# Seven-product up projection: relu on ScalarE, sums on VectorE, a fixed order on four engines, and the norm factor moved to the down sum

## The chip, the cores and the metric

One program on one core of a Trainium2 chip. The metric is the time of one execution on the device, in microseconds (us). The engines are called as the profile calls them: PE (TensorE matmul), PEld (its weight load), DVE (VectorE), ACT (ScalarE), POOL (GpSimd) and SP (SyncE, which issues nearly all DMA transfers here). Each engine works through its own instructions strictly in order, and they wait for each other on semaphores.

## The reference, cut to what matters

A trunk of two layers over 1040 positions of 1024 channels, batch 1, in float32. Layer 0 mixes by differential attention, layer 1 by a short convolution. Each mixer is followed by an MLP with 4096 hidden channels, and the change is in the MLP:

```python
def _rmsnorm(x, g):
    return x * lax.rsqrt(jnp.mean(x * x, -1, keepdims=True) + 1e-6) * g

def _sqrelu_mlp(h, w_up, w_down):
    a = jax.nn.relu(jnp.einsum('bld,df->blf', h, w_up))
    return jnp.einsum('blf,fd->bld', a * a, w_down)

for i in range(2):
    h = _rmsnorm(hres, norm_g[i, 0])
    m = mixer[i](h)                              # attention, then short convolution
    hres = hres + _rmsnorm(m, norm_g[i, 1])
    h = _rmsnorm(hres, norm_g[i, 2])
    hres = hres + _rmsnorm(_sqrelu_mlp(h, w_up[i], w_down[i]), norm_g[i, 3])
```

The factor of the norm in front of the MLP, written rs here, is one positive number for each position. The hidden value is (relu(u)·rs)² with u the projection of the unscaled row, and this equals relu(u)²·rs². So rs can be applied before the square, or rs² at any later point up to the sum over the hidden channels.

## The kernel before

Channels lie on the 128 partitions, positions along the free axis. A float32 product is made of three PE products of rounded parts: a value is split into `hi` (a rounded copy, made on ACT) and `lo` (the rest, subtracted on DVE), and PE sums hi·hi, hi·lo and lo·hi in PSUM.

The MLP of a layer (`mlp`) goes through these stages:

1. **Boundary groups** (`up_plain` with `boundary=True`): the first 4 of 32 hidden blocks of 128, by plain products, while the norm in front of the MLP is still being finished (`norm_step`, L390 to L393).
2. **Plain up groups** (`up_plain`): 4 more hidden blocks. Behind each product L465 takes relu and rs from PSUM to SBUF on DVE, L466 squares on ACT, L467 and L468 split, and two DMAs write the parts to `plain_dram`. Between the groups `turn` (called through `between`) forms sums and differences of the four quarters of the input by `sums` (L475 to L478) on POOL.
3. **Up by seven products** (`UpSevens`): the other 24 hidden blocks in 12 steps q, two blocks each. In a step seven products of half size take the place of eight (a Strassen-like scheme: rows and columns in halves, seven products of sums). The weights of a step come in two raw tiles (L526), POOL forms four sums of them (L534 to L537), ACT and DVE split them (L520, L521). The seven products go to the PSUM chains `a`, `b`, `c` (`ua`, `ub`, `uc`). Out of PSUM, three partial sums are copied by ACT (L603), the others added by DVE (L611); then relu and rs on DVE (L587, L606), square on ACT (L588, L607). The result is a tile `f` of eight slots; `finish` forms four sums of its slots on POOL (L571 to L574), since the down projection is done by seven products too, splits seven slots (L577 on ACT, L579 on DVE) and writes 14 parts to `seven_dram` (L578, L580). There are two buffers for f, called `two`, used by even and odd q in turn.
4. **Down plain**: the 4 plain up groups, loaded back into `stage` (L835), times four weight tiles, g = 0 to 3 (`load_weights`, `down_plain`, PE L188 `dn`). L841 copies out of PSUM into the accumulator `acc`, whose two tiles lie in the memory of the two f buffers.
5. **Down by seven products** (`Sevens`): 24 steps in 6 blocks b of 4. The operands of block 0 go to tiles `HH` and `HL` in layer 0, `YHa`, `YHb` and `HL` in layer 1 (`load`, L676), those of later blocks to `fx` and the same tiles in turn. L767 adds each product to `acc` on DVE.
6. The boundary groups' part of the down sum, with the last norm.

What sets the order: within one engine the order is the scheduler's, which places instructions by their readiness and by the order of the program text; inside the blocks `tc.manual_schedule(engines={PE})` of `UpSevens.run` and `Sevens.run` PE alone follows the text. All DMAs here are issued by SP in one order, and a DMA whose source is not ready holds those behind it. Names with a number such as `w_raw_11529` are tiles; `[waits ...]` lists the engines and DMA channels (DMAHW0 to DMAHW7) that an instruction waits for.

## Time and profile before

| | before |
|---|---|
| median of 3 runs | 2464.67 us (2463.58 to 2465.43) |
| profiled execution: its own time | 2467.3 us |
| profiled execution: span of the core | 2465.5 us |
| PE busy | 2315.0 us, 94% |
| DVE, ACT, POOL busy | 1644.1, 1114.4, 771.0 us |
| DMA moved | 374.63 MB |

The trace comes from the profiled execution, whose span lies 1.8 us inside its own time. Times inside the trace are counted from the start of the span. The seven-product up stage runs from about 727 to 998 us in layer 0 and from about 1832 to 2104 us in layer 1; the plain down stage follows it for some 60 us, and the seven-product down stage after that.

Where rows of the "stretches" view are quoted, the columns are: stretch, its length, then busy us and instructions of PE, PEld, DVE, ACT and POOL, then the clock granted to PE, the share of the DMA engines and GB/s. In the "waits" view a row has the engine and line that waits, what it waited for, the sum in us, the number of times and the longest.

### The profile page before, as it was taken

The page shows a single profiled execution, that of the slowest core. Times are in us where ns is not written, and L with a number is a line of the kernel's source. Part 1 is how long each engine was busy: PE and PEld are TensorE (multiplying, and loading weights), DVE is VectorE, ACT ScalarE, POOL GpSimd, SP SyncE. Part 2 cuts the span into 40 slices and gives each one's busy share as a digit, 9 for nine tenths or more (in the row PEclk, how much of TensorE's full clock was granted, in tenths as well). Part 3 has the DMA queues.
Part 4 walks back from the last instruction along what each step waited for, and adds up shares of the span by engine and source line. Part 5 has one row for each costly group of instructions (what it writes and reads, how often), then busy time and mean ns, then how long its engine had stood idle before and what let it go on. Part 6 is the DMA issues. An engine that isn't in the chain of part 4 may idle for free. (4 is left out here: it accounts for less than half of the span.)

```text
span 2465.5 us, 38542 instructions
## 1 busy us (share of the span) xinstructions
PE 2315.0 (94%) x14474; PEld 2162.6 (88%) x14474; DVE 1644.1 (67%) x2815; ACT 1114.4 (45%) x2141; POOL 771.0 (31%) x662
## 2 busy tenths in 40 slices
PE   8999999999889988799999999999899988899997
PEld 7899999999889988799999899999777666688887
DVE  7887777755977677267666944423976667367766
ACT  6777777765545455322123522224544445322224
POOL 3211111105614445133324200004624555133326
PEclk9999999999999999899999999999999999899998
DMA  4212222432445665875733311122445666876652
GB/s 133 63 55 61 61 61 61 146 106 90 133 144 173 217 213 203 324 281 198 276 131 102 128 50 46 46 73 72 135 154 173 217 215 210 313 284 221 246 196 69
DMA packets 168779, 374.63 MB, mean 152 GB/s; under 512 B 17040, under 2 KB 73744, under 8 KB 168080
## 3 DMA queue, kind: packets, MB, share of 16 engines
q1 hardware_dynamic: 168592, 372.17, 44.0%
q8 instruction: 114, 1.87, 0.3%
q14 instruction: 73, 0.60, 0.1%
HBM read 234.34 MB, written 129.24 MB: 147 GB/s over the span
## 5 line engine op out<-in xcount | busy, mean ns | idle before, releaser
L151 DVE TENSOR_TENSOR w_lo<-w_raw,w_hi 128x1024 fp32r<-128x1024 f32 (+1 forms) x63 | 82.6, 1313 | 153.1 <-ACT w_hi L150 153.0
L213 POOL TENSOR_TENSOR mss<-mss,sq 128x344 f32<-128x344 f32 (+2 forms) x42 | 50.1, 1197 | 375.8 <-ACT sq L212 372.6
L150 ACT CAST w_hi<-w_raw 128x1024 fp32r<-128x1024 f32 (+2 forms) x87 | 89.8, 1033 | 154.2 <-DMA w_raw<-in_wall 64.9
L722 POOL TENSOR_TENSOR s_tmp<-w_raw 128x256 f32<-128x256 f32 x48 | 35.7, 745 | 391.4 <-DVE s_lo L715 234.6
L188 PE MATMUL up<-HL,w_hi 128*128 128x344 f32 (+3 forms) x352 | 120.9, 345 | 9.4 <-DVE HL L393 9.4
L521 DVE TENSOR_TENSOR us_lo<-t,us_hi 128x1024 fp32r<-128x1024 f32 x48 | 60.6, 1263 | 100.7 <-ACT us_hi L520 100.6
L714 ACT CAST s_hi<-s_tmp 128x1024 fp32r<-128x1024 f32 x48 | 50.4, 1050 | 163.6 <-PE pb L744 154.4
L151 POOL TENSOR_TENSOR w_lo<-w_raw,w_hi 128x1024 fp32r<-128x1024 f32 (+1 forms) x24 | 57.5, 2395 | 196.6 <-ACT w_hi L150 183.9
L1396 ACT ACTIVATE E<-E,mn 16x16 f32<-16x16 f32 (+5 forms) x144 | 105.3, 732 | 24.1 <-DVE mn L1391 23.5
L188 PE MATMUL dn<-stage,w_hi 128*128 128x344 f32 (+2 forms) x320 | 91.0, 372 | 24.3 <-ACT w_hi L150 19.7
L188 PE MATMUL mo<-HL,w_hi 128*128 128x342 f32 (+2 forms) x312 | 99.9, 320 | 0.0
L1391 DVE CUSTOM_DVE_ANT_0 E<-s,G 16x16 f32<-16x16 f32 (+5 forms) x144 | 64.4, 455 | 39.9 <-PE s L1387 37.4
L188 PEld LDWEIGHTS dn<-stage,w_hi 128*128 128x128 f32 x320 | 61.5, 203 | 32.7 <-ACT w_hi L150 20.4
L579 DVE TENSOR_TENSOR f<-f,fhi 128x512 fp32r<-128x512 f32 x84 | 74.1, 931 | 22.7 <-ACT fhi L577 22.7
L714 ACT CAST a_hi<-w_raw 128x512 fp32r<-128x512 f32 x48 | 29.8, 620 | 129.5 <-DMA w_raw<-in_wall 126.8
L767 DVE TENSOR_TENSOR acc<-acc,pa 128x512 f32<-128x512 f32 x96 | 65.8, 686 | 33.5 <-PE pa L744 31.7
L188 PEld LDWEIGHTS up<-HL,w_hi 128*128 128x128 f32 x352 | 68.0, 193 | 16.4 <-DVE HL L393 13.0
L534 POOL TENSOR_TENSOR t<-w_raw 128x512 f32<-128x512 f32 x24 | 31.6, 1315 | 148.6 <-DMA w_raw<-in_wall 119.8
L715 DVE TENSOR_TENSOR s_lo<-s_tmp,s_hi 128x1024 fp32r<-128x1024 f32 x48 | 58.8, 1224 | 23.6 <-ACT s_hi L714 23.6
L562 PE MATMUL ua<-x,us_hi 128*128 128x256 f32 (+2 forms) x288 | 67.2, 326 | 7.7 <-ACT us_hi L520 2.1
L520 ACT CAST us_hi<-t 128x1024 fp32r<-128x1024 f32 x48 | 50.1, 1046 | 52.5 <-POOL t L535 46.1
L1139 PE MATMUL q<-HH,w_hi 128*128 128x348 f32 (+1 forms) x192 | 65.1, 339 | 6.5 <-ACT w_hi L150 6.5
(716 smaller groups left out, 9205.6 us busy)
## 6 DMA issues: line engine op xcount, KB each, us to landing
w_raw<-in_wall SPq DMA_DIRECT2D x189, 512.0 KB, 3.7
seven_dram<-fhi SPq DMA_DIRECT2D x84, 257.0 KB, 4.3
fx<-seven_dram SPq DMA_DIRECT2D x42, 514.0 KB, 7.2
seven_dram<-fhi SPq DMA_DIRECT2D x84, 256.0 KB, 2.7
seven_dram<-f SPq DMA_DIRECT2D x84, 256.0 KB, 4.7
fx<-seven_dram SPq DMA_DIRECT2D x42, 512.0 KB, 6.9
HH<-seven_dram SPq DMA_DIRECT2D x21, 514.0 KB, 7.7
HL<-seven_dram SPq DMA_DIRECT2D x21, 514.0 KB, 8.3
```

The lines of the kernel that those rows point to most:

```text
L150: nc.scalar.copy(hi_part, raw[:, cols])
L151: (eng or nc.vector).tensor_sub(lo_part, raw[:, cols], hi_part.bitcast(F32))
L188: nc.tensor.matmul(ps, lhs[:, a:b], rhs(k, cols), start=n == 0, stop=n == last)
L521: nc.vector.tensor_sub(hl[1], src, hl[0].bitcast(F32))
L562: nc.tensor.matmul(ps[:, off : off + n], lhs[:, a : a + P], self.operand(slot, t, j)[:, c : c + n], start=first and k == 0, stop=k == 11, ...
L579: nc.vector.tensor_sub(v[slot].bitcast(F32R), v[slot], hi.bitcast(F32))
L714: nc.scalar.copy(hl[0], src)
L715: nc.vector.tensor_sub(hl[1], src, hl[0].bitcast(F32))
L767: nc.vector.tensor_add(am, am, got)
L1139: nc.tensor.matmul(ps, wh[:, a], self.HH[:, k, s], start=k == 0, stop=False)
L1391: nc.vector.tensor_tensor_reduce(out=e[:rows, p0 : p0 + n], in0=ps[:rows], in1=self.G[:rows, off : off + n], scale=-(2.0 ** -(h + 1)), sca ...
L1396: nc.scalar.activation(e[:rows, :ext], e[:rows, :ext], AF.Exp, scale=-1.0, bias=mn, accum_out=H["sums"][:rows, c : c + 1])
```

## The change

It has seven parts.

1. In `UpSevens.run` the fixed order of the program text now holds for PE, ACT, DVE and POOL, where it held for PE alone. The text is rewritten so that the work on the tile of step q−1 and the stores of steps q−2 and q−1 are spread over the products of step q.
2. Relu moves from DVE (with rs) to ACT (without rs), in the plain up groups and in the steps q < 10. The boundary groups and the steps 10 and 11 keep rs. In exchange rs² is formed once after the up stage, and 16 products on DVE per layer (`nc.vector.tensor_mul(am, am, rs2...)`) scale the accumulator in the last steps of down block 4, which is behind all that lacks rs and ahead of all that has it.
3. The four sums of f's slots, and `turn`'s sums, move from POOL to DVE.
4. The second raw weight tile has two places (the second is `spare`, a tile of the norm that is free by then), both halves are fetched at the start of a step, and the four weight sums come in two pairs.
5. The stores of a tile are issued one by one in fixed places, no longer all after `finish`.
6. The two f buffers are taken once for the stage (`f586a` and `f586b` in layer 0), no longer anew in each step.
7. Down plain: the weights of g = 0 and 1 are loaded and split, and g = 2 loaded, ahead of the loads of `stage`; g = 3 follows after g = 0; the operands of block 0 are loaded two slots after each g.

```diff
@@ up_plain
-                    nc.vector.scalar_tensor_tensor(r, ps, 0.0, rs[:, s], ALU.max, ALU.mult)
+                    if boundary:
+                        nc.vector.scalar_tensor_tensor(r, ps, 0.0, rs[:, s], ALU.max, ALU.mult)
+                    else:
+                        nc.scalar.activation(r, ps, AF.Relu)
@@ UpSevens
-            sums(nc.gpsimd, t1, t3, t4, t2)
+            sums(nc.vector, t1, t3, t4, t2)
...
+        def fetch(self, q):
+            raws = []
+            for half in range(2):
+                i = self.base + 2 * q + half
+                if half and q % 2:
+                    raw = self.raws[1][:, :1024]
+                else:
+                    raw = (self.wu if half else wp).tile([P, 1024], F32, tag="w_raw", name=f"w_raw{i}", bufs=1)
+                nc.sync.dma_start(raw, wall[i])
+                raws.append(raw)
...
+            if step == 0:
+                nc.gpsimd.tensor_add(t[:, n:], a21, a22)
+                nc.gpsimd.tensor_sub(t[:, :n], t[:, n:], a11)
+            else:
+                nc.gpsimd.tensor_sub(t[:, :n], a11, a21)
+                nc.gpsimd.tensor_sub(t[:, n:], a12, self.W[q]["t21"][:, :n])
...
-            nc.gpsimd.tensor_sub(v[3], v[7], v[0])
-            nc.gpsimd.tensor_sub(v[2], v[5], v[3])
-            nc.gpsimd.tensor_sub(v[4], v[5], v[7])
-            nc.gpsimd.tensor_sub(v[6], v[1], v[2])
-            for slot in (0, 3, 5, 4, 2, 1, 6):
...
+        def store(self, q, slot):
+            x = self.v[q % 2][:, slot]
+            hi = self.fp.tile([P, self.H], F32R, tag="hi", name=f"fhi{q}_{slot}_{count[0]}", bufs=4)
+            nc.scalar.copy(hi, x)
+            nc.sync.dma_start(self.spool[q][:, slot, 0], hi.bitcast(F32))
+            nc.vector.tensor_sub(x.bitcast(F32R), x, hi.bitcast(F32))
+            nc.sync.dma_start(self.spool[q][:, slot, 1], x)
...
+            def closed(slot, q):
+                at, z = {1: (0, 0), 4: (5, 1), 5: (7, 1), 6: (1, 0)}[slot]
+                x = self.v[q % 2][:, at]
+                src = sums[slot, q] if slot == 6 else x
+                if q < 2 * (NW - 1):
+                    nc.scalar.activation(x, src, AF.Relu)
                 else:
+                    nc.vector.scalar_tensor_tensor(x, src, 0.0, self.rs[:, z * H : (z + 1) * H], ALU.max, ALU.mult)
+                nc.scalar.activation(x, x, AF.Square)
...
-            with tc.manual_schedule(engines={mybir.EngineType.PE}):
+            with tc.manual_schedule(engines={ET.PE, ET.Activation, ET.DVE, ET.Pool}):
                 step(0, 0)
+                for q in range(n + 2):
+                    if more:
+                        self.fetch(q + 1)
                     step(4, q - 1)
+                    if 0 < q < n:
+                        self.settle(q, "s21")
+                    self.store(q - 2, 2)
                     step(5, q - 1)
+                    added(4, q - 1)
+                    self.store(q - 2, 1)
+                    closed(4, q - 1)
+                    step(1, q)
+                    held(0, q)
+                    added(5, q - 1)
+                    self.store(q - 2, 6)
+                    closed(5, q - 1)
+                    step(6, q - 1)
+                    added(1, q)
+                    if more:
+                        self.settle(q + 1, "a")
+                        self.combine(q + 1, 0)
+                    closed(1, q)
+                    sub(q - 1, 3, 7, 0)
+                    step(2, q)
+                    closed(6, q - 1)
+                    sub(q - 1, 4, 5, 7)
+                    sub(q - 1, 2, 5, 3)
+                    self.settle(q, "s34")
+                    step(3, q)
+                    held(2, q)
+                    sub(q - 1, 6, 1, 2)
+                    self.store(q - 1, 0)
+                    self.store(q - 1, 3)
+                    if more:
+                        self.combine(q + 1, 1)
+                    step(0, q + 1)
+                    held(3, q)
+                    self.settle(q, "d")
+                    self.store(q - 1, 5)
+                    self.store(q - 1, 4)
@@ Sevens.run
                 nc.vector.tensor_add(am, am, got)
+                if slot in (1, 4, 5, 6) and q // 4 == NW - 2:
+                    nc.vector.tensor_mul(am, am, rs2[:, z * H : (z + 1) * H])
@@ mlp
-        up.run(m)
+        up.run()
+        rs = rs[:, :W]
+        nc.vector.tensor_mul(rs, rs, rs)
...
+        ws, split, slots = [weights(), weights()], load_weights(), iter(range(7))
         for c0, n in chunks:
             for i in range(2):
                 nc.sync.dma_start(f[i][:, :, s].bitcast(F32), plain[1][:, i * FB : (i + 1) * FB, s])
-        for slot in range(7):
-            seven.load(0, slot)
         for g in range(FB):
-            down_plain(acc, *f, [g], chunks, lambda mi, cols, am, ps: nc.scalar.copy(am, ps))
+            w = ws[g]
+            down_plain(acc, *f, [g], chunks, lambda mi, cols, am, ps: nc.scalar.copy(am, ps), [[(w, 0), (w, FB * P)]])
+            for slot in (next(slots, None) for _ in range(2)):
+                if slot is not None:
+                    seven.load(0, slot)
+            if split:
+                ws.append(split())
+                split = load_weights() if g == 0 else None
```

Here `sub(q, out, a, b)` subtracts slot b from slot a of the tile of step q on DVE, `held` is the copy of a partial sum on ACT, and `added` the addition of a product on DVE, both as before.

**In the steady state of the up stage**, POOL had the four sums of f between the weight sums. Before, in layer 0:

```order
L571 TENSOR_TENSOR f_2a<-f_2a 128x514 [waits DMAHW1_49,DMAHW5_49,DMAHW0_49,Activation_49]
L573 TENSOR_TENSOR f_2a<-f_2a 128x514
L572 TENSOR_TENSOR f_2a<-f_2a 128x514 [waits Pool_49]
L574 TENSOR_TENSOR f_2a<-f_2a 128x514 [waits Activation_49,Pool_49]
L534 TENSOR_TENSOR t_4_597_9354<-w_raw_9352 128x512 [waits DMAHW4_49,DVE_49]
L536 TENSOR_TENSOR t_4_597_9355<-w_raw_9191,w_raw_9352 128x512 [waits DMAHW2_49,DVE_49]
L535 TENSOR_TENSOR t_4_597_9354<-t_4_597_9354,w_raw_9191 128x512 [waits Pool_49]
L537 TENSOR_TENSOR t_4_597_9355<-w_raw_9191,t_4_597_9354 128x512 [waits Pool_49]
```

After, the same sums stand on DVE (L634), among the additions from PSUM (L617), the splits of the weights (L527) and the splits of f (L591):

```order
L617 TENSOR_TENSOR f586b<-f586b,uc_9236 128x514 [waits PE_49]
L527 TENSOR_TENSOR ua_lo_597_9296<-w_raw_9167,ua_hi_597_9295 128x1024 [waits DMAHW7_49,Activation_49]
L634 TENSOR_TENSOR f586a<-f586a 128x514 [waits DMAHW6_49]
L634 TENSOR_TENSOR f586a<-f586a 128x514 [waits DMAHW4_49]
L634 TENSOR_TENSOR f586a<-f586a 128x514 [waits DVE_49]
L527 TENSOR_TENSOR us_lo_597_9334<-t_3_595_9124,us_hi_597_9333 128x1024 [waits Activation_49]
L634 TENSOR_TENSOR f586a<-f586a 128x514 [waits DMAHW2_49,DVE_49]
L591 TENSOR_TENSOR f586a<-f586a,fhi_0_598_9364 128x514 [waits Activation_49]
L591 TENSOR_TENSOR f586a<-f586a,fhi_3_598_9369 128x514 [waits Activation_49]
```

The sums have left POOL and now stand in DVE's fixed order, one tile behind the additions.

**At the end of the up stage in layer 0**, SP issued the last stores of the tile of step 10 (`f_10a`) ahead of the loads of `stage` (L835) and of block 0 (L676). Before:

```order
L578 DMA seven_dram_81<-fhi_6_621_11345 128x514 [waits DMAHW5_49,Activation_49]
L580 DMA seven_dram_81<-f_10a 128x514 [waits DMAHW6_49,DVE_49]
L580 DMA seven_dram_81<-f_10a 128x514 [waits DMAHW7_49,DVE_49]
L580 DMA seven_dram_81<-f_10a 128x514 [waits DMAHW0_49,DVE_49]
L578 DMA seven_dram_81<-fhi_0_622_11489 128x514 [waits DMAHW1_49,Activation_49]
L835 DMA stage_11529<-plain_dram_1_78 128x4x344 [waits DMAHW2_49,PE_49]
```

After, the last two parts of that tile (slot 6, from `fhi_6` and `f586a`) stand behind the loads of `stage` (L887; the last of them is the first row) and behind eight loads of block 0 (L721):

```order
L887 DMA stage_11514<-plain_dram_1_78 128x4x340 [waits DMAHW5_49]
L721 DMA HH<-seven_dram_81 128x1028 [waits DMAHW6_49,PE_49]
L721 DMA HL<-seven_dram_81 128x1028 [waits DMAHW7_49]
L721 DMA HH<-seven_dram_81 128x1028 [waits DMAHW0_49,PE_49]
L721 DMA HL<-seven_dram_81 128x1028 [waits DMAHW1_49]
L721 DMA HH<-seven_dram_81 128x1028 [waits DMAHW2_49]
L721 DMA HL<-seven_dram_81 128x1028 [waits DMAHW3_49]
L721 DMA HH<-seven_dram_81 128x1028 [waits DMAHW4_49,PE_49]
L721 DMA HL<-seven_dram_81 128x1028 [waits DMAHW5_49]
L590 DMA seven_dram_81<-fhi_6_622_11436 128x514 [waits DMAHW6_49,Activation_49]
L592 DMA seven_dram_81<-f586a 128x514 [waits DMAHW7_49,DVE_49]
L721 DMA HH<-seven_dram_81 128x1028 [waits DMAHW0_49]
```

The store of slot 6 has moved from ahead of these loads to behind most of them; in layer 1 it stands behind all 14 loads of block 0 and a weight load.

**On ACT at the same place** the first copy of the plain down stage (L890, which was L841) waits for that store, since `acc0a` lies in the memory of `f586a`:

```order
L589 CAST fhi_3_622_11478<-f586b 128x514 [waits DMAHW7_49,Activation_49]
L589 CAST fhi_5_622_11483<-f586b 128x514 [waits DMAHW1_49,Activation_49]
L589 CAST fhi_4_622_11488<-f586b 128x514 [waits DMAHW6_49,DVE_49,Activation_49]
L890 COPY acc0a<-dn_11537 128x344 [waits DMAHW5_49,DMAHW2_49,DMAHW7_49,DMAHW0_49,PE_49]
L890 COPY acc0a<-dn_11551 128x344 [waits PE_49]
```

All further copies of the first accumulator tile, the splits of the weights of g = 2 and 3 and the last splits of f stand behind that one wait on ACT.

More of the change, by code (lines that the diff above doesn't have):

```diff
@@ L614, in run, with held, added @@
-            with tc.manual_schedule(engines={mybir.EngineType.PE}):
+                sums[slot, q] = self.product(tiles[chain, q], slot, q, first)
+            def held(slot, q):
+                if 0 <= q < n:
+                    nc.scalar.copy(self.v[q % 2][:, {0: 0, 2: 7, 3: 5}[slot]], sums[slot, q])
+            def added(slot, q):
+                if 0 <= q < n and slot != 6:
+                    x = self.v[q % 2][:, {1: 0, 4: 5, 5: 7}[slot]]
+                    nc.vector.tensor_add(x, x, sums[slot, q])
@@ L831, in mlp @@
         f = quarters(st, W)
+        seven = Sevens(wd, H, base, spool)
+        acc = [two(i, f"acc{layer}") for i in range(2)]
+        ws, split, slots = [weights(), weights()], load_weights(), iter(range(7))
         for c0, n in chunks:
@@ L852, in after_base @@
                     nc.sync.dma_start(f.bitcast(F32), plain[0][:, i * FB : (i + 1) * FB])
[L854 removed]
+            seven.run(acc, [[sevens(t, H)[:, k] for k in range(7)] for t in fx], after_base, rs)
         reopen()
```

107 lines of the change are left out of this document (34 added, 73 removed).

## The prediction

> **What bounds the kernel now.** I read the page first: its engine rows, then the stretches by stage, then PE's waits in the stages that the change touches, then the durations of the operations that it moves.
>
> ```profile
> PE 2315.0 (94%) x14474; PEld 2162.6 (88%) x14474; DVE 1644.1 (67%) x2815; ACT 1114.4 (45%) x2141; POOL 771.0 (31%) x662
> ```
>
> PE is the bound overall, so a gain is to be had only where PE stands still. The stretches show where:
>
> ```profile
> 636.00:670.00 34.00, 28.63 (x167) 26.85 (x165) 33.97 (x43) 19.00 (x30) 25.18 (x21) 0.95 0.32 115
> 727.00:998.00 271.00, 252.03 (x2016) 248.65 (x2016) 190.54 (x210) 131.89 (x208) 126.11 (x89) 0.97 0.60 201
> 732.00:792.00 60.00, 60.00 (x504) 60.00 (x504) 36.84 (x41) 28.02 (x43) 22.60 (x16) 1.00 0.45 153
> 998.00:1036.00 38.00, 25.20 (x146) 24.66 (x147) 7.15 (x9) 10.14 (x20) 4.17 (x3) 0.85 1.04 390
> 1036.00:1060.00 24.00, 24.00 (x149) 24.00 (x148) 7.66 (x8) 9.13 (x19) 7.03 (x8) 0.95 0.28 93
> 1100.00:1160.00 60.00, 60.00 (x505) 60.00 (x504) 42.82 (x61) 12.75 (x19) 19.99 (x24) 1.00 0.65 244
> 1831.00:2104.00 273.00, 245.03 (x1013) 190.00 (x1011) 193.30 (x221) 136.19 (x213) 132.89 (x89) 0.98 0.60 207
> 1850.00:1888.00 38.00, 38.00 (x165) 30.78 (x164) 25.05 (x28) 18.31 (x29) 17.18 (x11) 1.00 0.41 140
> 2104.00:2139.00 35.00, 24.69 (x97) 19.28 (x98) 7.55 (x9) 9.74 (x16) 4.63 (x4) 0.88 1.03 403
> 2139.00:2164.00 25.00, 25.00 (x97) 19.97 (x97) 7.89 (x8) 8.64 (x15) 7.05 (x8) 0.89 0.33 108
> ```
>
> The up stage by seven products (727 to 998, 1831 to 2104) has PE idle or slow in both layers, though its own first part (732 to 792) runs without a gap. The seven-product down stage (1100 to 1160) has no gap to win. What PE waits for, first in layer 0's up stage (727 to 998), then in layer 1's, then in front of layer 1's (1740 to 1831):
>
> ```profile
> PE ua L562 <- DVE r L465: 10.1, 1, 10.1
> PE ua L562 <- ACT fhi L577: 8.0, 6, 2.3
> PE ua L562 <- ACT f_11b L603: 4.5, 2, 3.2
> ...
> PE ua L562 <- ACT f L603: 17.2, 11, 5.6
> ...
> PE up L188 <- DVE HL L393: 4.7, 6, 1.2
> PE up L188 <- DVE w_lo L151: 3.6, 1, 3.6
> ```
>
> L603 is the copy that empties a PSUM bank. The view of that line in layer 1 tells why it is late:
>
> ```profile
> L603 ACT COPY f<-ua x23: 567/581/589, 1844.8 to 2092.7; 128x512 f32<-128x512 f32 x23
>   DMA seven_dram<-fhi: 21.7, 4
>   DMA seven_dram<-f: 20.1, 6
> ```
>
> ACT sat idle for 41.8 us in front of this copy because the stores of the tile two steps earlier still read the buffer. They come in one burst after `finish`, whose sums POOL makes slowly.
>
> **The up stage.** Dense pace: in layer 0, 60.00 us / 504 = 0.119 us a matmul, so 2016 matmuls take 240.0; the stretch has 271.0, so 31.0 too much. I keep 1.9 (the first 5 us after the cold start, below) and 0.7 (the stage's first wait for `stage` lies inside): **−28**. In layer 1, 38.00 / 165 = 0.230, for 1013 matmuls 233.3 of 273.0: 39.7 too much. About 1.9 of it is the stage's start and 0.9 the wait for `stage`; since a few records can be missing, I take 2 less again: **−35**.
>
> Is the new steady state dense? It has to fit in 84 × 0.230 = 19.3 us a step in layer 1, 20.0 in layer 0, on each engine. Durations, layer 1, each row min/median/max:
>
> ```profile
> L579 DVE TENSOR_TENSOR f<-f,fhi x77: 674/679/1789, 1861.7 to 2095.5; 128x512 fp32r<-128x512 f32 x77
> L588 ACT ACTIVATE f<-f x35: 626/633/637, 1843.6 to 2099.4; 128x512 f32<-128x512 f32 x35
> L521 DVE TENSOR_TENSOR us_lo<-t,us_hi 128x1024 fp32r<-128x1024 f32 x23 | 29.2, 1268 | 53.8 <-ACT us_hi L520 53.8
> L521 DVE TENSOR_TENSOR ua_lo<-w_raw,ua_hi 128x1024 fp32r<-128x1024 f32 x11 | 21.5, 1950 | 6.9 <-ACT ua_hi L520 6.9
> L520 ACT CAST us_hi<-t 128x1024 fp32r<-128x1024 f32 x23 | 24.1, 1049 | 29.2 <-POOL t L535 25.7 <-PE ub L562 1.8 <-POOL t L537 1.6
> L572 POOL TENSOR_TENSOR f<-f 128x512 f32<-128x512 f32 x11 | 25.0, 2275 | 0.0
> L534 POOL TENSOR_TENSOR t<-w_raw 128x512 f32<-128x512 f32 x24 | 31.6, 1315 | 148.6 <-DMA w_raw<-in_wall 119.8
> ```
>
> Per step, *DVE*: 7 splits of f, 3 additions, 4 new sums and one small weight split at 0.68 = 10.2, and three large weight splits of 1.27, 1.27 and 1.95 = 4.5: 14.7. The four relu leave. *ACT*: 7 splits and the small weight split at 0.62, 3 copies at 0.58, 4 squares and 4 relu at 0.63 (a relu on ACT is not in the trace; below it stands the copy from PSUM, 0.58, above it twice the square, 1.27, which would add 2.6), 3 large splits at 1.05: 14.9, at most 17.5. *POOL*: 4 × 1.32 = 5.3, since the sums of f (up to 2.28 each) leave. All are under 19.3. The cover of every one of these edits is PE itself; where the fixed order makes an engine wait with something ready behind it, the cover has 4 to 5 us on DVE and ACT. Waits remain at the two last steps (relu with rs on DVE) and at the end, where nothing is behind. I take **+3** for both layers, of 0 to +24 (1 us in each of 24 steps).
>
> DVE and POOL slow each other: 0.68 becomes 1.79 at worst in L579's row. POOL's work falls from about 12 to 5.3 us a step, so this shrinks. The Trainium skill, "SBUF — State Buffer", Terms, says that the two share a port pair, exclusively, and that the loser fully blocks for the whole instruction. By that rule DVE would lose up to 5.3 a step on top of durations that partly hold it already, 20.0 in place of 14.7, and layer 1 would be bound by DVE by 0.7 × 12 = 8 us, an estimate that gives 2409; the trace agrees that they exclude each other, but not that every overlap is a full loss, as the median of L579 is its minimum.
>
> **In front of the up stage.** PE waited in layer 1 for HL and w_lo 8.3 us by the rows above, and in layer 0 for less; DVE was busy 33.97 of 34 us (636 to 670). `turn` puts 16 sums of about 0.68 on it, 11 us per layer. In return POOL's sums no longer slow it:
>
> ```profile
> L393 DVE SCALAR_TENSOR_TENSOR HL<-m,g,YHb x8: 561/1159/1583, 1741.5 to 1771.1; 128x342 fp32r<-128x342 f32 x4, 128x340 fp32r<-128x340 f32 x4
> L468 DVE TENSOR_TENSOR fr<-fr,fh x11: 503/505/1603, 1748.8 to 1799.8; 128x342 fp32r<-128x342 f32 x8, 128x340 fp32r<-128x340 f32 x3
> ```
>
> Some 8 + 6 operations were longer by 0.6 to 1.1 each, and a handful of the casts beside them: 10 to 15 us. The sums stand behind the last HL, so HL comes earlier. I take −5 for layer 1 and −1 for layer 0, **−6** of 0 to −10. The wait of 10.1 (`r` L465) at the start of layer 0's stage is the last `up` bank, which waits for a buffer still read by the stores to `plain_dram`. A relu on ACT does not free that buffer: **0** (−3 to +3).
>
> **Plain down.** Here DMA is full (share 1.04 and 1.03), and PE waited for the weights of g = 2, behind all of block 0:
>
> ```profile
> PE dn L188 <- ACT w_hi L150: 11.5, 1, 11.5
> PE dn L188 <- DMA stage<-plain_dram: 1.9, 2, 1.2
> ...
> PE dn L188 <- ACT w_hi L150: 8.2, 1, 8.2
> PE dn L188 <- DMA stage<-plain_dram: 2.7, 2, 1.8
> ...
> seven_dram<-fhi SPq DMA_DIRECT2D x84, 257.0 KB, 4.3
> HH<-seven_dram SPq DMA_DIRECT2D x21, 514.0 KB, 7.7
> stage<-plain_dram SPq DMA_DIRECT2D x4, 688.0 KB, 7.3
> ```
>
> The reordered loads remove that wait. But another is late next: the first copy to `acc` (L890 after) waits for the store of slot 6 of step 10, which SP now issues behind `stage` and eight loads of block 0. By bytes in layer 0, from the first stores of step 10 on: 14 stores × 0.257, 6 loads of `stage` (4.1), 8 × 0.514 and a weight tile 0.5, 12.3 MB; at 0.39 MB/us 32 us. They begin three products (8.6 us) before the up stage ends at time T, so the store lands at T+23. PE fills the four PSUM banks, 24 / 149 × 12 = 1.9 us each, and after some 3 us of waiting for `stage` stands from T+11 to T+23. Behind L890 on ACT are all other copies and the last splits. Total 288 × 0.161 = 46.4, + 3 + 12 = 61, as long as before (62): **0** (−12 to +4). In layer 1: 14 × 0.256 + 4.1 + 14 × 0.512 + 1.0 = 15.9 MB at 0.40 land at T+31; seven banks of 25 / 97 × 12 = 3.1 and 4 of waiting last until T+26, so a stall of 5, and 192 × 0.258 + 4 + 5 = 58.5 against 60: **−2** (−8 to +4).
>
> **The norm factor in the down sum.** 16 products on DVE per layer, near the addition L767 with 0.68, make 11 us in four down steps of 84 × 0.119 = 10 us. DVE is busy 42.82 of 60 there, so 28.5 + 11 of 40: just full. **+2** for both layers (0 to +6). rs² itself runs while DVE is idle.
>
> **The sum**: −28 −35 +3 −6 +0 −2 +2 = −66. Against the profiled execution's own 2467.3 us (1.8 over its span): **2401 us**; that execution lies 2.6 above the median of the runs, which I leave inside the range.
>
> **The rivals.**
> - *The new wait on `acc` is hidden*: if the store goes out sooner than its place by bytes, plain down gains about 11 and 8 more: 2384. For it: POOL is gone from the chain that makes slot 6. Against it: SP's order is fixed, and DMA is full there.
> - *The fixed order loses time in each step*: an engine waits for an instruction that its text has too early, 1 us in each step, +24: 2425. For it: four engines and no scheduler. Against it: 4 to 5 us of room.
> - *Slow matmuls after short gaps stay.* PE's idle time in the two stretches is 271.00 − 252.03 = 19.0 and 273.00 − 245.03 = 28.0, 47 in all, but 71 were too much; the other 24 is PE busy at a slower pace (granted clock 0.97 and 0.98 there). If that pace has another cause than the gaps, only the gaps go, 47 − 3.5 in place of 63: 2421. Against it: the dense stretches (732 to 792, 1850 to 1888) run at 1.00 throughout. The Trainium skill, "TensorE: Matmul & The Clock Gate", Part 1, has the clock halve only after an idle window of about 3.4 us; most waits here are shorter (2.3 at the longest in the row of `fhi`), so its rule speaks for this case.
> - *Slower*: slot 0 of a tile is stored after product 3 of a step and overwritten by the held copy four products later, some 11 us. ACT stands at that copy if the stores land later than that, and in the fixed order everything is behind it. Each us over 11 costs 24 us; from 14 on the gain is gone, and at 15 the kernel takes about 2490. Against it: stores land in 4.3 us at the median with DMA at 0.60.
> - *No effect*: the stores still hold the tiles, and the waits only change their names: 2465.
>
> **How the numbers follow.** Forecast 0.57, hidden wait 0.13, lossy order 0.12, slow matmuls 0.08, no effect 0.04, slower 0.06. The range takes in the first four cases with the bounds of the down terms: 2376 to 2432. Faster by over 0.2% (about what a measurement can tell from no change): 0.90; within it 0.04; slower 0.06.
>
> **What would show it.** The up stages take 242 to 246 and 236 to 240 us, with no L603 copy (now `held`) waiting for a store. PE's waits at plain down name the copy to `acc` behind `seven_dram<-f`, 12 and 5 us, in place of `w_hi`. DVE is near 98% in down block 4. I am wrong if PE waits in every up step, or if plain down takes under 52 us.

## The result, and the profile after

| | before | changed |
|---|---|---|
| median | 2465.05 us (2463.58 to 2468.35, 4 runs) | 2392.27 us (2388.80 to 2394.41, 4 runs) |
| profiled execution: own time, span | 2467.3, 2465.5 us | 2388.8, 2386.9 us |
| ratio | 1 | 0.9702, 95% interval 0.9685 to 0.9718 |

The change takes 3.0% off. Of the page after, the engine rows, as before:

```profile
span 2386.9 us, 38367 instructions
PE 2293.7 (96%) x14474; PEld 2156.5 (90%) x14474; DVE 1635.3 (69%) x2877; ACT 1166.0 (49%) x2241; POOL 596.3 (25%) x534
```

The stretches of the changed kernel, with the same columns as before: the two seven-product up stages, each followed by its plain down stage.

```profile
713.00:956.00 243.00, 241.54 (x2017) 241.33 (x2017) 181.08 (x214) 155.38 (x249) 67.24 (x44) 1.00 0.63 215
956.00:1023.00 67.00, 49.93 (x288) 48.99 (x289) 18.43 (x23) 20.60 (x42) 7.14 (x8) 0.87 0.78 283
1787.00:2019.00 232.00, 231.67 (x999) 187.23 (x997) 180.14 (x213) 155.92 (x249) 67.70 (x44) 1.00 0.63 219
2019.00:2085.00 66.00, 51.03 (x204) 40.13 (x205) 18.33 (x25) 19.55 (x34) 6.64 (x8) 0.90 0.80 307
```

PE now works through both up stages without a gap (the 1.5 us missing from the first stretch lie ahead of its first product and behind its last), at a granted clock of 1.00 where it was 0.97 and 0.98. DVE has 181 us in 12 steps, 15.1 a step; ACT has 12.9 and POOL 5.6. The plain down stages have not gained: PE is busy 49.93 of 67 and 51.03 of 66 us. What PE waits for from layer 0's up stage to the end of its plain down, and then the same in layer 1:

```profile
PE dn L188 <- ACT acc0a L890: 10.6, 1, 10.6
PE dn L188 <- DVE f586b L628: 3.7, 1, 3.7
PE dn L188 <- DMA stage<-plain_dram: 3.3, 2, 2.6
PE ua L578 <- ACT r L470: 1.5, 1, 1.5
...
PE dn L188 <- ACT acc L890: 12.9, 1, 12.9
PE dn L188 <- DMA stage<-plain_dram: 2.4, 3, 1.4
```

The wait for the copy to `acc` has come. Two views tell how. ACT's timeline in layer 0 (start, length, instruction, and in brackets how long ACT was idle before it and what ended that):

```profile
959.95 0.62 ACT L589 CAST fhi<-f586a 128x514 fp32r<-128x514 f32 x1 [6.21 <-DMA seven_dram<-fhi]
961.94 0.63 ACT L629 ACTIVATE f586b<-f586b 128x514 f32<-128x514 f32 x1 [1.36 <-DVE f586b L628]
963.93 0.63 ACT L629 ACTIVATE f586b<-f586b 128x514 f32<-128x514 f32 x1 [1.36 <-DVE f586b L628]
964.47 1.65 ACT L589 CAST fhi<-f586b 128x514 fp32r<-128x514 f32 x3
981.97 0.62 ACT L589 CAST fhi<-f586b 128x514 fp32r<-128x514 f32 x1 [15.85 <-DMA seven_dram<-fhi]
982.61 1.49 ACT L890 COPY acc0a<-dn 128x344 f32<-128x344 f32 x4
```

And the DMAs that SP issued there (start, length, instruction):

```profile
970.88 0.32 SPq L721 DMA_DIRECT2D HL<-seven_dram  x1
972.20 0.32 SPq L590 DMA_DIRECT2D seven_dram<-fhi  x1
973.49 0.32 SPq L592 DMA_DIRECT2D seven_dram<-f586a  x1
974.73 0.32 SPq L721 DMA_DIRECT2D HH<-seven_dram  x1
```

ACT stands 15.85 us at the cast of slot 4 of step 11, since all four `hi` buffers are taken: one of them holds slot 6 of step 10 (cast at 959.95), whose store SP issues only at 972.20, behind eight loads of block 0, and which has landed by 981.97. The four copies to `acc` stand behind that cast and follow at once.

The stages side by side, from the traces. 0 and 1 are the layers, each row is one traced execution. "Front" runs from the first boundary product to the first product of the up stage, "down" is the seven-product down stage; where a plain down product stands among the last up products, the border of the two is uncertain by 4 us, their sum is not.

| us | front 0 | up 0 | plain down 0 | down 0 | front 1 | up 1 | plain down 1 | down 1 |
|---|---|---|---|---|---|---|---|---|
| before | 119.1 | 270.4 | 62.2 | 242.2 | 108.2 | 271.4 | 60.6 | 239.5 |
| changed | 106.7 | 241.5 | 67.6 | 243.6 | 99.7 | 235.5 | 62.3 | 239.5 |
| stores_only | 118.1 | 243.0 | 62.7 | 242.3 | 108.2 | 239.0 | 52.2 | 244.5 |
| before_sums | 118.8 | 251.3 | 63.7 | 242.5 | 108.9 | 246.5 | 60.2 | 239.5 |
| before_relu | 118.4 | 262.0 | 62.6 | 243.6 | 108.2 | 256.7 | 59.5 | 239.5 |
| order_pe | 108.9 | 244.8 | 60.3 | 243.0 | 101.4 | 233.9 | 53.1 | 240.3 |
| relu_dve | 112.5 | 257.1 | 66.8 | 242.6 | 100.5 | 253.9 | 61.5 | 239.5 |
| sums_pool | 111.1 | 242.5 | 72.7 | 243.6 | 99.5 | 242.0 | 62.9 | 239.5 |
| turn_pool | 115.6 | 242.9 | 68.0 | 243.6 | 108.3 | 236.5 | 61.5 | 239.5 |
| down_old | 105.6 | 243.1 | 68.5 | 244.0 | 99.8 | 235.5 | 61.9 | 239.6 |
| base_behind10 | 106.4 | 241.7 | 64.6 | 243.7 | 101.2 | 235.5 | 54.6 | 240.2 |
| base_behind11 | 106.5 | 241.4 | 56.4 | 253.3 | 106.7 | 235.5 | 47.7 | 247.0 |
| loads_split_tail | 111.7 | 241.4 | 57.9 | 243.5 | 105.8 | 235.4 | 44.7 | 241.1 |
| order_pe_loads | 107.5 | 243.9 | 46.1 | 243.1 | 101.5 | 233.9 | 44.9 | 244.2 |

### The profile page after: what moved, and what is told of

Its sections match the earlier page's. It is cut to its first block, busy times and chain, and to the rows that moved or that the text cites. A ratio compares the mean times of both kernels' runs of the same rounds, so it can differ in the third digit from the quotient of the medians.

```text
span 2386.9 us, 38367 instructions
## 1 busy us (share of the span) xinstructions
PE 2293.7 (96%) x14474; PEld 2156.5 (90%) x14474; DVE 1635.3 (69%) x2877; ACT 1166.0 (49%) x2241; POOL 596.3 (25%) x534
## 5 line engine op out<-in xcount | busy, mean ns | idle before, releaser
L213 POOL TENSOR_TENSOR mss<-mss,sq 128x344 f32<-128x344 f32 (+2 forms) x42 | 50.0, 1196 | 374.8 <-ACT sq L212 371.6
L188 PE MATMUL dn<-stage,w_hi 128*128 128x344 f32 (+2 forms) x320 | 92.2, 370 | 32.9 <-ACT acc L890 12.9
L591 DVE TENSOR_TENSOR f<-f,fhi 128x512 fp32r<-128x512 f32 x84 | 80.2, 981 | 25.9 <-ACT fhi L589 25.8
L527 DVE TENSOR_TENSOR us_lo<-t,us_hi 128x1024 fp32r<-128x1024 f32 x48 | 58.6, 1220 | 24.8 <-ACT us_hi L526 24.8
L1494 DVE TENSOR_TENSOR AL<-tr,AH 128x512 fp32r<-128x512 f32 (+4 forms) x120 | 63.9, 543 | 8.2 <-ACT AH L1493 7.6
L789 PE MATMUL pa<-fx,s_hi 128*128 128x256 f32 (+2 forms) x288 | 65.6, 320 | 0.6 <-DVE acc0b L812 0.6
L188 PE MATMUL cg<-HH,w_hi 128*128 128x344 f32 (+1 forms) x192 | 62.9, 328 | 3.1 <-ACT HH L392 2.8
```

The source lines that it names most:

```text
L188: nc.tensor.matmul(ps, lhs[:, a:b], rhs(k, cols), start=n == 0, stop=n == last)
L591: nc.vector.tensor_sub(x.bitcast(F32R), x, hi.bitcast(F32))
L789: nc.tensor.matmul(ps[:, off : off + n], lhs[:, a : a + P], F[j][slot][:, t, c : c + n], start=first and k == 0, stop=k == 5, skip_group_c ...
L1494: nc.vector.tensor_sub(AL[:, j0 : j0 + nj, col : col + width], s, ah.bitcast(F32))
```

## The experiments

Medians are of four runs each; every ratio is to the kernel before, run on the same chip in the same session, with its 95% interval.

### One part alone: which part makes the up stage dense

**stores_only** keeps of the change the new text of the up stage (stores one by one, two places for the second weight tile, tiles taken once) and the reordered loads. The rest is undone.

```diff
-            sums(nc.vector, t1, t3, t4, t2)
+            sums(nc.gpsimd, t1, t3, t4, t2)
...
-                if q < 2 * (NW - 1):
-                    nc.scalar.activation(x, src, AF.Relu)
-                else:
+                if True:
                     nc.vector.scalar_tensor_tensor(x, src, 0.0, self.rs[:, z * H : (z + 1) * H], ALU.max, ALU.mult)
...
-                    nc.vector.tensor_sub(v[:, out], v[:, a], v[:, b])
+                    nc.gpsimd.tensor_sub(v[:, out], v[:, a], v[:, b])
...
-            with tc.manual_schedule(engines={ET.PE, ET.Activation, ET.DVE, ET.Pool}):
+            with tc.manual_schedule(engines={ET.PE}):
...
```

> The changed kernel with the fixed order for PE alone, relu and the norm factor on DVE, and the sums of f and of turn on GpSimd: of the change only the new text stays, with the stores one by one, the second raw weight tile, the two tiles taken once and the reordered loads. Theory A (the spread stores free the tile in time, which is what PE waited for): the up stages 245 to 260 us, total 2425 to 2445. Rival B (without the lighter DVE the scheduler's order comes out as before): up stages 265 or more, total 2455 or more.

Measured: 2403.18 us, 0.9750 (0.9735 to 0.9765). Theory A, and more of it than expected: the up stages take 243.0 and 239.0 us. Of PE's waits between 720 and 960 us and between 1800 and 2045 us one each is left, in layer 0 at the start of the stage and in layer 1 in its first step:

```profile
PE ua L575 <- DVE r L467: 8.8, 1, 8.8
...
PE ua L575 <- ACT f L609: 2.4, 1, 2.4
```

The spread stores were not taken apart from the rest of the new text. The second place for weights can have had little part in layer 0, where PE waited for weights only 0.8 us in the kernel before (5.3 us in layer 1):

```profile
PE ua L562 <- DVE us_lo L521: 0.8, 1, 0.8
```

**before_sums** and **before_relu** make the opposite test, one part of the change in the kernel before. (before_relu also has relu on ACT in the plain groups, and rs² in the down sum.)

```diff
@@ before_sums
-            nc.gpsimd.tensor_sub(v[3], v[7], v[0])
+            nc.vector.tensor_sub(v[3], v[7], v[0])
...
@@ before_relu
...
-            def close(x, z):
-                nc.vector.scalar_tensor_tensor(x, x, 0.0, self.rs[:, z * H : (z + 1) * H], ALU.max, ALU.mult)
+            def close(x, src, z, q):
+                if q < 2 * (NW - 1):
+                    nc.scalar.activation(x, src, AF.Relu)
+                else:
+                    nc.vector.scalar_tensor_tensor(x, src, 0.0, self.rs[:, z * H : (z + 1) * H], ALU.max, ALU.mult)
```

> The kernel before with one part of the change: the four sums of f on DVE in place of GpSimd. Theory A (the sums take 0.7 us in place of 1.5 to 2.3, so the burst of stores starts some 4 us earlier in each step and DVE is slowed less): the waits for L603 and fhi shrink by 1 us or more in each step, up stages 250 to 262 us, total 2435 to 2455. Rival B (DVE with relu and sums is the limit, as in relu_dve): the up stages as before or longer, total 2460 or more.

Measured: 2422.84 us, 0.9823 (0.9809 to 0.9838); up stages 251.3 and 246.5. Theory A, again with more than was expected: −19.1 and −24.9.

> The kernel before with one part of the change: relu on ACT in the plain groups and in steps 0 to 9, and the square of the norm factor in the down sum. Sums on GpSimd, stores in one burst, order and loads as before. relu_dve lost 15.6 and 17.3 us in the up stages by undoing this part. Theory A (what holds PE before is the burst of stores behind the slow sums; relu on ACT shortens it little): the up stages take 262 to 272 us each, total 2455 to 2468. Rival B (DVE's load is what made the chain late, and this part alone takes 36 relu of 0.9 us off it): 8 us or more less in each up stage, total 2450 or less.

Measured: 2440.35 us, 0.9900 (0.9885 to 0.9915); up stages 262.0 and 256.7, −8.4 and −14.7. Rival B, at its weak end.

Together these three say that the parts do not add up. In layer 0 the new text with the spread stores wins 27.4 us, the sums alone 19.1, relu alone 8.4, 55 in all, and the whole change wins 28.9. A reading that fits is that they all shorten the same loop: PE fills a bank, ACT and DVE empty it into a tile, the tile's sums are formed and its parts stored, and only then is the tile free two steps later. Once that loop is shorter than PE's own step, nothing more is to be had.

### One part taken out of the change

**order_pe** leaves the fixed order to PE alone.

```diff
-            with tc.manual_schedule(engines={ET.PE, ET.Activation, ET.DVE, ET.Pool}):
+            with tc.manual_schedule(engines={ET.PE}):
```

> The changed kernel with the fixed order in the up stage for PE alone, as before; the text, the stores one by one, the sums on DVE and relu on ACT stay. Theory A (the gain of 29 and 40 us in the two up stages comes from the work that left the slow chain and from the stores that are spread; DVE at 15.1, ACT at 12.9 and POOL at 5.6 us a step have room, and the scheduler starts from the same text): PE waits little, the up stages take at most 10 us more than now (242 and 231), total 2392 to 2404. Rival B (the fixed order itself carries the gain; the scheduler's order puts work for the next step ahead of what PE waits for): half or more of the 69 us comes back, total 2425 or more.

Measured: 2378.87 us, 0.9643 (0.9627 to 0.9659), some 13 us faster than the changed kernel. Theory A for the up stages (244.8 and 233.9 with the border's uncertainty). The sign of the total was not expected: up and plain down together take 305.1 and 287.0 where the changed kernel has 309.1 and 297.8. In the scheduler's order SP issues the last store of step 10 at 958.8 us, ahead of the loads of block 0, 1.4 us before the last product of the up stage; in the changed kernel it goes out 18 us behind that product. The first copy to `acc` starts at 967.9 in place of 982.6, and the wait for the first accumulator tile shrinks from 10.6 to 1.5. In layer 0 a wait for the second tile is left:

```profile
PE dn L188 <- ACT acc0b L890: 11.3, 1, 11.3
PE dn L188 <- ACT acc0a L890: 1.5, 1, 1.5
```

**relu_dve** puts relu and the norm factor back on DVE in one operation, in the plain groups and in all steps, and drops the products with rs² and the square of the factor.

```diff
-                    if boundary:
-                        nc.vector.scalar_tensor_tensor(r, ps, 0.0, rs[:, s], ALU.max, ALU.mult)
-                    else:
-                        nc.scalar.activation(r, ps, AF.Relu)
+                    nc.vector.scalar_tensor_tensor(r, ps, 0.0, rs[:, s], ALU.max, ALU.mult)
...
-                if q < 2 * (NW - 1):
-                    nc.scalar.activation(x, src, AF.Relu)
-                else:
+                if True:
...
-                if slot in (1, 4, 5, 6) and q // 4 == NW - 2:
-                    nc.vector.tensor_mul(am, am, rs2[:, z * H : (z + 1) * H])
...
```

> The changed kernel with relu and the norm factor back on DVE in one operation (plain groups and all up steps), and without the 16 products and the square of the factor. DVE then has 15.1 + 4 x 0.69 = 17.9 us of a step of 19.3 to 20. Theory A (relu on ACT is not what makes the up stage dense; DVE would still fit): the up stages within 6 us of 242 and 231; the seven-product down stage of layer 0 is 1.4 us shorter; the wait at the start of layer 0's up stage (10.1 before, 1.5 now, 7.2 with turn's sums on GpSimd) comes back by at most 3 us; total 2388 to 2400. Rival B (DVE is the limit once the sums are on it, with its slowing by GpSimd): 1 to 3 us more in each step, total 2416 or more.

Measured: 2424.54 us, 0.9833 (0.9813 to 0.9854); up stages 257.1 and 253.9, 15.6 and 18.4 more than changed. The size is rival B's, its reason is not: DVE is busy 213 of 250 us in layer 0's stage, 85%. There PE waits nine times, seven of them for DVE's relu of slot 6, which empties a bank of the chain that the next step starts in. The rows of relu_dve, and at the end the stretch of stores_only:

```profile
722.00:972.00 250.00, 237.98 (x1962) 236.37 (x1962) 213.04 (x248) 127.36 (x205) 72.63 (x44) 0.99 0.60 201
PE ua L575 <- DVE f586b L623: 5.8, 4, 1.7
PE ua L575 <- DVE f586a L623: 4.1, 3, 1.5
...
728.00:970.00 242.00, 242.00 (x2012) 241.96 (x2012) 209.03 (x209) 131.98 (x208) 134.85 (x87) 0.99 0.65 219
```

In the fixed order that relu stands in DVE's line among sums and splits. stores_only, with relu on DVE too but the scheduler's order there, has no such wait, though DVE is as busy, 209 of 242 us (with slower operations, as the sums of f are on GpSimd there). So it is rather the fixed order that needs relu on ACT than DVE's load; the scheduler's order with relu and sums both on DVE was not run. In layer 1 the eight waits, 10.1 us, name ACT's copy of a partial sum instead.

**sums_pool** puts f's sums back on GpSimd.

```diff
-                    nc.vector.tensor_sub(v[:, out], v[:, a], v[:, b])
+                    nc.gpsimd.tensor_sub(v[:, out], v[:, a], v[:, b])
```

> The changed kernel with the four sums of f back on GpSimd, in the same places of its fixed order; all else as changed. By load GpSimd has 4 x 1.32 + 4 x 1.5 to 2.3 = 12 to 14 us of a step of 19.3, DVE 2.7 us less. Theory A (load decides, and there is room): the up stages stay within 6 us of 242 and 231, total 2388 to 2402. Rival B (the slow chain of sums is what held the stores and so the tile; the fixed order also makes DVE's splits wait for them in line): PE waits in each step, 1 to 3 us, total 2416 to 2464.

Measured: 2406.71 us, 0.9755 (0.9740 to 0.9769), between the two. Layer 0's up stage does not change (242.5), layer 1's takes 6.5 more; plain down in layer 0 takes 5 more, with the copy to `acc` 22.3 us late, and the front of layer 0 takes 4.4 more by a wait of 5.6 us that the last section describes. relu_dve has that wait too (6.6 us in layer 0).

**turn_pool** puts `turn`'s sums back on GpSimd.

```diff
-            sums(nc.vector, t1, t3, t4, t2)
+            sums(nc.gpsimd, t1, t3, t4, t2)
```

> The changed kernel with the sums of turn back on GpSimd, all else as changed. Between the start of the boundary groups and the start of the seven-product up stage the change won 12.3 us in layer 0 (8.6 of them the wait of 10.1 us at its end, now 1.5) and 8.3 in layer 1. Theory A (the sums on GpSimd slow DVE, which delays HL, w_lo and the splits of the plain groups): PE's waits for HL and w_lo come back, 3 to 4 us in layer 0 and 7 to 9 in layer 1, and the wait at the end stays short, since relu on ACT made it so; total 2402 to 2406. Rival B (the wait of 10.1 us was late for the sums too): it comes back as well, total 2410 to 2416. Rival C (the sums on DVE cost as much as they win): total within 4 us of 2392.

Measured: 2410.27 us, 0.9773 (0.9757 to 0.9789); the fronts take 115.6 and 108.3 us, 8.9 and 8.6 more than changed. Rival B in the total: beside HL and w_lo the wait at the start of layer 0's up stage comes back with 7.2 of its 10.1 us. ACT's relu stands 11.2 us there for the stores that free its buffer, 5.7 in the changed kernel. PE between 600 and 730 us:

```profile
PE ua L578 <- ACT r L470: 7.2, 1, 7.2
PE sum L204 <- DVE q L197: 3.8, 3, 1.9
PE up L188 <- DVE HL L393: 3.8, 6, 0.9
PE up L188 <- DVE w_lo L151: 1.8, 1, 1.8
```

### The plain down stage

**down_old** has the loads of plain down in the order of before (part 7 undone: the loads of `stage`, then block 0, then each weight tile ahead of its products).

```diff
-        ws, split, slots = [weights(), weights()], load_weights(), iter(range(7))
...
+        for slot in range(7):
+            seven.load(0, slot)
         for g in range(FB):
-            w = ws[g]
-            down_plain(acc, *f, [g], chunks, lambda mi, cols, am, ps: nc.scalar.copy(am, ps), [[(w, 0), (w, FB * P)]])
...
+            down_plain(acc, *f, [g], chunks, lambda mi, cols, am, ps: nc.scalar.copy(am, ps))
```

> The changed kernel with part 7 undone: the loads of plain down and of block 0 in the order of before, all else as changed. Theory A (the late store of step 10 comes from the stores being spread past the end of the up stage, not from the reordering of loads): PE still waits 8 us or more for the copy to acc in each layer, and the wait for the weights of g = 2 (11.5 and 8.2 us before) comes back in part; total 2392 to 2406 us. Rival B (the reordering made the stores late): plain down takes 62 and 60 us as before, total 2378 to 2384.

Measured: 2394.51 us, 0.9708 (0.9690 to 0.9726). Theory A, but for the wait for weights, which does not come back: PE waits 16.7 and 14.0 us for the copy to `acc`, and the weights of g = 2 are ready by then. The reordering of loads is worth nothing that these runs can tell while that wait stands.

**base_behind10** and **base_behind11** have SP issue block 0's loads behind the last store of step 10, or of step 11. `stored` keeps the DMA of each store; the second kernel has `- 1` for `- 2`.

```diff
...
                 if slot is not None:
-                    seven.load(0, slot)
+                    with tc.issue_after(up.stored[2 * NW - 2, 6].ins):
+                        seven.load(0, slot)
```

> As base_behind11, but the loads of down block 0 are put only behind the last store of step 10; the stores of step 11 stay among and behind them. Theory A: the wait of the first copy to acc goes (10.6 and 12.9 us), and since the second accumulator tile lies in the memory of step 11's tile, a shorter wait of 0 to 8 us appears at its first copy; total 2368 to 2380 us. Rival B: total within 6 us of 2392. Rival C (the order of stores 10 alone does not matter, the four hi buffers hold ACT until the stores of step 11 land): the first copy to acc is still 8 us or more late, total 2385 or more.

Measured: 2382.10 us, 0.9665 (0.9646 to 0.9684). The first copy to `acc` is 2.1 us late in place of 10.6 (theory A, against C); in layer 0 the second tile's copy is 6.2 late, in layer 1 the weights of g = 3 are 5.4 late. The total is 2 us above A's range.

> The changed kernel with one edit: SP issues the 14 loads of down block 0 behind the last store of step 11, no longer ahead of the last stores of steps 10 and 11. Theory A (the new wait at plain down is the last store of step 10 standing in SP's queue behind these loads; in the trace of the changed kernel ACT waits 15.9 and 13.2 us for it at the cast of fhi, and PE then 10.6 and 12.9 us for the copy to acc): both waits of PE go, plain down takes 54 to 57 us in layer 0 (67 now) and 52 to 55 in layer 1 (66 now), the total is 2366 to 2372 us. Rival B (DMA is full there anyway, so whatever is put back is late in turn: w3, or block 0 at the start of the seven-product down stage): a wait of 8 us or more appears at one of these in each layer, and the total stays within 6 us of 2392.

Measured: 2384.76 us, 0.9669 (0.9650 to 0.9689). Both theories hold in part: plain down takes 56.4 and 47.7 us, 11 and 15 less, but the down stage takes 253.3 and 247.0, 10 and 7 more. The wait in layer 0 is for the split of the weights of the stage's third step. SP issues them at 1022.5 us (1010.8 in the changed kernel), behind the 14 loads of block 1 to `fx`, and at the first of these SP stood 16.5 us until PE was done with `stage`, in whose memory `fx` lies. So it is block 1, more than block 0, that they stand behind. In layer 1 the front has 6.6 us of the wait of the last section. PE from 700 to 1060 us:

```profile
PE pa L789 <- ACT a_hi L759: 7.1, 1, 7.1
...
PE dn L188 <- ACT acc0a L890: 1.4, 1, 1.4
```

**loads_split_tail** splits those loads around the first weights of the down stage, and puts the last three stores of step 10 behind the last relu of step 11.

```diff
...
+        with tc.issue_after(up.stored[2 * NW - 1, 6].ins), tc.issue_after(raw_loads[-1].ins):
+            for slot in range(3):
+                seven.load(0, slot)
         seven.fetch(0)
+        with tc.issue_after(raw_loads[-1].ins):
+            for slot in range(3, 7):
+                seven.load(0, slot)
...
                     closed(6, q - 1)
+                    if q == n:
+                        for slot in (2, 1, 6):
+                            self.store(q - 2, slot)
```

Here `raw_loads[-1]` is the last weight DMA traced: that of g = 3 in the first place, that of the down stage's first step in the second.

> The changed kernel with its tail reordered: the loads of down block 0 stand behind the last store of step 11 and the weights of g = 3 (three slots), and behind the first weights of the seven-product down stage (four slots); the last three stores of step 10 stand behind the last relu of step 11 on ACT and DVE. In base_behind11 the waits of 10.6 and 12.9 us went, but 10 and 7 us came back in the seven-product down stage, whose first weights stood behind all of block 0; and 3.7 us in layer 0 are a PSUM bank held by step 11, whose relu stands on ACT behind the cast of slot 6. Theory A (each of these is a place in a queue and can be moved; the bytes fit): plain down 50 to 55 us in layer 0 and 49 to 53 in layer 1, the down stage as in the changed kernel (243.5 and 228.5), total 2360 to 2370. Rival B (the bytes do not fit: what is moved back is late): 8 us or more of waits at w3, at the first products of the down stage, or at later slots; total 2378 or more.

Measured: 2370.55 us, 0.9611 (0.9597 to 0.9625). Theory A, half a us beyond its range: plain down 57.9 and 44.7, the down stage 243.5 and 241.1. In layer 0 PE's wait for the copy is 3.2, that for `stage` 4.8, and none is left for `f586b`. The fronts hold 6.6 and 5.5 us of the wait of the last section, so the tail itself has won more than the total shows.

**order_pe_loads** has the same split of the loads (not the moved stores) in order_pe.

> The changed kernel with the fixed order for PE alone (as order_pe) and the loads of down block 0 behind the last store of step 11, in two parts as in loads_split_tail. In order_pe PE waits 11.3 us in layer 0 for the copy to the second accumulator tile and 4.5 in layer 1 for the weights of g = 3, both behind block 0's loads. Theory A (these are places in SP's queue): both go, plain down 50 to 54 us in layer 0 and 48 to 51 in layer 1, total 2358 to 2367. Rival B (the up stages, 241 and 234 with the scheduler's order, or the first weights of the down stage pay for it): total 2370 or more.

Measured: 2359.76 us, 0.9574 (0.9558 to 0.9590). Theory A: both waits go, and the total is the lowest of all, 1.3% below the changed kernel. (loads_split_tail, 11 us above it, has 12.1 us of the wait of the last section, and this kernel none.) Plain down takes 46.1 and 44.9 us, less than expected; PE hardly stands still there. Its stretches, up stage and plain down of layer 0, then of layer 1:

```profile
714.00:958.00 244.00, 242.80 (x2016) 242.63 (x2017) 172.84 (x216) 155.22 (x251) 64.44 (x43) 0.99 0.65 220
958.00:1005.00 47.00, 46.00 (x296) 45.72 (x295) 13.37 (x18) 18.48 (x37) 5.74 (x8) 1.00 0.98 360
1771.50:2005.50 234.00, 234.00 (x1010) 189.45 (x1009) 172.03 (x216) 155.54 (x251) 64.79 (x43) 1.00 0.64 227
2005.50:2050.50 45.00, 45.00 (x195) 36.12 (x194) 13.99 (x20) 17.19 (x30) 5.57 (x8) 1.00 0.97 374
```

DMA is nearly full in plain down (0.98 and 0.97), and PE's clock is at 1.00: the bytes fit, it was their order that did not.

## Why the prediction was right, and where it was not

The profiled execution took 78.5 us less, 66 were forecast (the medians are 72.8 apart); the measured median, 2392, lies in the range of 2376 to 2432. The main mechanism, the up stages that become dense, was right. The other terms missed in both directions: the front won 15 us more than forecast, and plain down came out 9 worse. That these partly cancel is luck.

- **The up stages**, −28 and −35 with +3 for waits that stay: PE's two stretches are full at 241.54 of 243.00 and 231.67 of 232.00 us, with no waits left. By the table layer 0 goes from 270.4 to 241.5, −28.9, and layer 1 from 271.4 to 235.5, −35.9 (−40 if the border is set ahead of the last 12 up products, which stand behind the first of plain down). DVE's load was right, 14.7 us a step forecast and 15.1 measured; ACT's was 2 too high, 14.9 and 12.9. The reason was right in kind (the burst of stores and POOL's sums held the tile). The working did not say which edits it needs: stores_only shows that the new text with the spread stores was nearly enough.
- **In front of the up stage**, −6, and 0 for the wait of 10.1: measured −12.4 and −8.5, 20.9 in all. The step that failed is "A relu on ACT does not free that buffer: **0**", which looked at relu alone: the wait shrank from 10.1 to 1.5, 8.6 us. Relu alone does bring little (8.8 are left in before_relu). But the wait is 7.2 in turn_pool, 5.6 in order_pe and 3.0 in relu_dve, so `turn`'s sums have the largest part in that gain, and the fixed order one too; neither was thought of for this wait. In turn_pool and order_pe ACT's relu stands longer for the stores to `plain_dram`, 11.2 and 10.2 us against 5.7; what holds these stores was not followed further. The rest, 12.3, is twice the −6 forecast: the relief of DVE was mis-sized, in layer 0 above all (−1 forecast, −3.8 measured; its HL and w_lo cost 7.1 before and 2.7 after).
- **Plain down**, 0 and −2: measured +5.4 and +1.7 by the table (67.6 against 62.2, 62.3 against 60.6; +6 in layer 1 by the other border). The store and its place in SP's queue were named rightly; its price of 12 us was 10.6 in layer 0, and in layer 1 it was 12.9, not 5. In layer 0 the sum 46.4 + 3 + 12 became 49.9 + 7.0 + 10.6: PE is slower here (granted clock 0.87), and of the 7.0 us, 3.7 are the bank held by step 11's relu, which was left out. In layer 1 the stall was mis-sized because PE stood from 21 us behind the last up product, not 26. The store landed some 27 and 33 us behind that product, not 23 and 31; from 951 us on DMA was full as the working had it, but not in the six us before:

```profile
945.00:948.00 3.00, 3.00 (x27) 3.00 (x26) 1.88 (x4) 1.89 (x4) 0.00 (x0) 1.00 0.68 186
948.00:951.00 3.00, 3.00 (x27) 3.00 (x26) 3.00 (x5) 2.69 (x6) 0.00 (x0) 1.00 0.81 229
951.00:982.00 31.00, 14.47 (x84) 13.32 (x82) 10.03 (x16) 4.10 (x8) 0.00 (x0) 0.82 1.05 387
```

  The last link was another, too: it is not the copy that waits for the store of f's low part, but a cast ahead of it in ACT's line that waits for the buffer which the store of the `hi` part frees.
- **The norm factor**, +2: the down stages take +1.4 and 0. In block 4 of layer 0, DVE is busy 36.20 of 40 us, 90%, not 98%, and PE waits 0.4:

```profile
1184.00:1224.00 40.00, 39.63 (x328) 39.18 (x328) 36.20 (x52) 8.21 (x12) 15.48 (x16) 1.00 0.44 166
```

- **The rivals.** The hidden wait did not come. The lossy order did, in another place: nothing in the steps, but 13 us in the tail (order_pe), where the fixed order has the last store of step 10 issued behind loads of block 0. (By its own rate the *slower* case at 15 us is 2401 + 4 × 24 = 2497, not 2490.) Slow matmuls did not stay: the up stages won 65 us by the table, though PE's idle time in them was 47, so in this kernel the slower pace went with the gaps. Its first part is the clock: by the granted 0.97 and 0.98 it makes 0.03 × 271 + 0.02 × 273, some 14 of the 24 us of slow pace; the rest was not traced to a cause. Four stretches before the change, the first of them the start of the stage, from which the 1.9 us kept in the forecast comes (5.00 − 26 × 0.119), and the first product behind a gap of 2.26 us (in brackets, what ended it), 1.3 us ahead of the second stretch:

```profile
727.00:732.00 5.00, 5.00 (x26) 5.00 (x27) 3.71 (x3) 0.32 (x1) 3.22 (x3) 0.57 0.38 135
827.00:830.00 3.00, 3.00 (x16) 3.00 (x15) 3.00 (x4) 1.64 (x4) 0.73 (x1) 0.50 1.00 249
940.00:942.50 2.50, 2.50 (x14) 2.50 (x13) 2.50 (x3) 1.89 (x5) 1.35 (x1) 0.50 0.55 211
1841.00:1844.00 3.00, 3.00 (x8) 2.32 (x8) 2.97 (x4) 0.36 (x1) 2.84 (x3) 0.50 0.47 175
825.72 0.36 PE L562 MATMUL ua<-HH,ua_hi 128*128 128x258 f32 x1 [2.26 <-ACT fhi L577]
```

  The other two half-clock stretches follow gaps of 2.71 and 1.83 us. The Trainium skill ("TensorE: Matmul & The Clock Gate", Part 1) has the clock halve after an idle window of about 3.4 us; here it was halved behind shorter gaps, and the measurement decides.
- The full lock of the Trainium skill ("SBUF — State Buffer", Terms) would have given DVE 20.0 us a step; 15.1 were measured, so that loss did not come in the steady state. One that may be of its kind came elsewhere, below.

## What to carry to other kernels

When several slow things lie on one loop that frees a buffer, price the loop, not its parts: here the new text with the spread stores brought nearly all of the gain in the up stage, and the single gains of three edits added up to nearly twice the whole. A fixed order on an engine ties the work of the next stage to the last work of this one, so its price is read at the seam, where buffers are reused and DMA is full. There, ask of each store which buffer it frees and what SP issues ahead of it: moving 14 loads behind two tiles' stores, and eight of them behind the next weights, brought 17 us by the ratios (order_pe to order_pe_loads) without touching any arithmetic.

## What the runs showed of the hardware that was not expected

With `turn`'s sums on DVE, one addition on GpSimd (L213, the sum of squares of the norm) can take 12.9 us in place of 0.95 (the median), and PE waits for it. The view of that line in base_behind11, layer 1 (min/median/max in ns):

```profile
L213 POOL TENSOR_TENSOR ssn<-ssn,sq x14: 897/945/12862, 1697.5 to 1741.9; 128x342 f32<-128x342 f32 x7, 128x340 f32<-128x340 f32 x7
  PE sum L204: 6.6, 1
```

While that addition stands (1728.99 to 1741.86 us), DVE runs 21 operations back to back, `turn`'s sums and the splits of the boundary groups, from 1729.96 to 1741.10; the addition ends 0.8 us behind that row. In the trace of the changed kernel the same two last additions take 1.1 and 1.3 us, and it is two sums on DVE that take 1.4 in place of 0.68. PE's wait, 5.5 to 6.6 us, is in the traces of base_behind11, loads_split_tail, sums_pool and relu_dve, at one or both layers, and not in that of the changed kernel, nor in any trace with `turn`'s sums on GpSimd (before, before_sums, before_relu, stores_only, turn_pool). GpSimd has the same two additions in base_behind11 and in the changed kernel, so I read it as a matter of which engine gets in first; this is not shown. The Trainium skill ("SBUF — State Buffer", Terms) says that the loser of the shared port pair blocks for the whole instruction; here, if that port is the cause, it was blocked for a row of them. What decides it was not tried.
